# A hybrid encoder step: the scan's eight quads taken in pairs behind a projection's end, whole matmul triples in the first 21 groups, and three smaller moves

## The chip, the cores and the metric

The kernel runs on one core of a Trainium2 chip. The metric is the device time of one execution in microseconds; the time of a kernel is the median of its runs. PE is TensorE (matmuls), ACT is ScalarE, DVE is VectorE, POOL is GpSimd, SP is SyncE, which issues most DMAs.

## The reference

One layer (DEPTH = 1) of a streaming encoder runs for two request groups with the same weights: 256 prompt frames and 32 sample frames, 288 token columns in all.

```python
xn   = rmsnorm(x, norm_mix_pre)
u, z, xbc, dt_raw = split(xn @ w_in)          # 2048 -> 1024 | 2048 | 2560 | 32
y_pool = pool_mixer(u)                        # trailing means of 2/4/8/16, minus u, @ w_pool, * pool_scale
xbc  = silu(causal_dwconv(xbc, width 4))      # -> xs (2048), B and C (2 groups x 128)
y    = scan(xs, softplus(dt_raw + bias), -exp(a_log), B, C) + D * xs    # 32 heads of 64
y_ssd = group_rmsnorm(y * silu(z)) * ssd_norm
x    = x + rmsnorm(concat[y_pool, y_ssd] @ w_out, norm_mix_post)
up   = causal_dwconv(rmsnorm(x, norm_ffn_pre) @ w_up, width 3)          # 2048 -> 2 x 5632
x    = x + rmsnorm((silu(gate) * value) @ w_down, norm_ffn_post)
```

It returns x for both groups and the new histories and scan states.

The exact scan of the prompt is computed here for each head as a masked product: with g the running sum of dt * A, token row s contributes exp(g_t - g_s) * (C_t . B_s) * dt_s * x_s to every later token t. The sample tokens take the same product over their own rows and a product with the old state.

## The kernel before

**Projections.** Each of the big products (w_in, w_out, w_up, w_down) is made by `project` in groups of 256 output columns. Tokens are the moving operand (288 columns), weights the stationary one. The weights come from HBM as `raw` (SP), ACT rounds them to a high half `whi`, and DVE subtracts to get the low half `wlo`; four buffers of each. The tokens are split in the same way. `mm3` makes one product of 128 x 128 weights as a triple of matmuls: high weights with high tokens, high weights with low tokens, low weights with high tokens. A weight *part* is what one whi/wlo tile feeds: 24 matmuls. A w_in group has 2048 rows and 256 columns, so four parts, 96 matmuls. Groups 1 to 8 are xs (the scan's input; B, C and two of the eight u tiles are made in the start stage), 9 to 16 are z, 17 to 19 are u, 20 to 25 are w_out (group 20 holds two column groups), and from 26 on come w_up and w_down. The table `TURNED` says for some groups in which of their parts the triple is turned (high-high, low-high, high-low).

**The scan.** The 32 heads are taken in eight *quads* of four. `ssd_first(q)` fetches the quad's row of running sums, broadcast to all partitions (`gb`, read from `g_d` by POOL), and the old state (`h0t`, SP), and makes `ce`, the decay towards the old state. `ssd_tokens(q)` reads the tokens transposed (`xk`, from `xs_d`). `ssd_quad(q)` scales xk by dt (DVE), makes the mask `m`: 12 ACT activations, one ACT exponential over all, one DVE product with `cbt` (the product of C and B), and then 16 float32 matmuls into two PSUM tiles `py`, one for each pair of heads, and two DVE additions of D * xs. `m`, `gb`, `ce` have two buffers, `xk` three. [...]

**Order.** The program is written by a tile scheduler: an instruction goes as early as its priority and the estimated readiness of its inputs allow; `pin` fixes matmuls in the order written, and the whi/wlo splits run ahead of their use by priority. `XS_RATE` and `Z_RATE` say behind which xs and z group a quad is written. Between matmuls that aren't pinned the scheduler may put others, so a quad's 16 may stand in the middle of a part and between the three matmuls of a triple.

**Start.** The first six column tiles (0 and 1 of u, 2 to 5 of B and C) are made from chunks of rows of `w_first` as they land, `CHUNKS` = six of one 128-row slice and five of two; `prepare` splits them into one tile `w` with the high and the low half, `W_GAP` elements apart. Twelve matmuls on `busy` run ahead of the first data. The sum of squares of the tokens is made by matmuls with a square of ones (`prs`).

Of the kernel before, what the change touches and what calls it, by code (L numbers as in the profile page):

```python
# [8 lines left out]
F32 = mybir.dt.float32  # L9
F32R = mybir.dt.float32r  # L10
# [6 lines left out]
P = 128  # L17
TC = {"schedule_with_timeline_sim": True}
D_MODEL = 2048
NP_ = 256  # L20
# [43 lines left out]
def body(  # L64
# [69 lines left out]
    def split_w(raw, kb, nk, nc_, after=()):  # L134
# [13 lines left out]
            out.append([(kb + k + i, hi[:, i, :], lo[:, i, :]) for i in range(n)])  # L148
        return out

    def mm3(out, wh, wl, a, start, stop, other=False):
        pairs = [(wh, 0), (wh, 1), (wl, 0)]
        if other:
            pairs[1:] = pairs[:0:-1]
        for n, (w, x) in enumerate(pairs):
            pe.matmul(out, w, a[:, x, :], start=start and n == 0, stop=stop and n == 2)  # L156

    groups_done = [0]

    def project(view, groups, acts, ksplit, before=None, done=None, spare=(), hold=(), behind=None, wait=(), tail=()):  # L160
# [7 lines left out]
        turned = TURNED.get(groups_done[0])  # L168
        n_part = 0
        after = before(*ksplit[0]) if before else None  # L170
        for i, (kb, n) in enumerate(ksplit):
            raws = [fetch_w(view, kb, n, c0, w) for c0, w in groups]
            nxt = None
            if before and i + 1 < len(ksplit):
                nxt = before(*ksplit[i + 1])
            m0 = 0
            for raw, (c0, w) in zip(raws, groups):
                parts = split_w(raw, kb, n, w, tuple(wait) + ((after or ()) if m0 else ()) + (hold if i else tail if m0 + w // P == n_all else ()))
                for q, part in enumerate(parts):
                    for m in range(w // P):  # L180
                        c = slice(m * P, (m + 1) * P)
                        with ExitStack() as order:
                            if behind and part[-1][0] == k_last and m0 + m > SUMS_AFTER:
                                order.enter_context(tc.issue_after(behind[-1].ins))
                            for k, hi, lo in part:
                                mm3(accs[m0 + m], hi[:, c], lo[:, c], acts[k], k == k_first, k == k_last, n_part == turned)
# [22 lines left out]
    busy = xin.tile([P, 2 * P], F32R, name="busy")  # L209
    pin(dve.memset(busy.bitcast(F32), 1.0))  # L210
    win = w_in
    O_Z, O_X = D_POOL, D_POOL + D_SSD
# [39 lines left out]

    ones = const.tile([P, P], F32, name="ones")
    pool.memset(ones, 1.0)
    eps_t = side1.tile([P, 1], F32, name="eps_t")
    pool.memset(eps_t, EPS)
    warm = const.tile([P, 1], F32, name="warm")
# [26 lines left out]
        pin(pe.matmul(first[1][:, : 2 * P], busy[:, 0:P], busy, start=True, stop=True))  # L284
    last_split = []
    lows = []
    sq2 = xin.tile([P, 2 * NT], F32, name="sq2")

    def prepare(i):

# [53 lines left out]
    for i, (kb, n) in enumerate(CHUNKS):  # L344
        if i + 1 < len(CHUNKS):
            ahead_w.append(prepare(i + 1))
            for q in SQUARES.get(i + 1, ()):
                squares(q)
        if i == 5:
            first_load(10)  # L350
            pin(dve.memset(ebuf[0][:, 0:1], 0.0))
# [12 lines left out]
        products = [  # L364
            (r, m, k, x) for m in (2, 3, 4, 5, 0, 1) for k in range(n) for r, x in ((0, 0), (0, 1), (1, 0))
        ]
        if i == 0:
            products.sort(key=lambda q: (q[1] < 2, q[0], q[3]))
        for q, (r, m, k, x) in enumerate(products):
            if i == len(CHUNKS) - 2 and q == 24:  # L370
                p_ = aux([P, NT], "prs")
                for c in (slice(0, NT), slice(NT, 2 * NT)):
                    pin(pe.matmul(p_, busy[:, 0:P], sq_r[:, c], start=c.start == 0, stop=c.start > 0))
# [5 lines left out]
            pin(pe.matmul(  # L379
                first[m], w[r][:, k, m * P : (m + 1) * P], xn[kb + k][:, x, :],  # L380
                start=kb + k + r + x == 0, stop=kb + k == KD - 1 and r == 1,
            ))
# [26 lines left out]
    ones_r = const.tile([P, P], F32R, name="ones_r")  # L409
    pin(act.activation(ones_r, ones, AF.Copy))  # L410
    sc_stage = const.tile([P, 2, 3, NXC], F32, name="sc_stage")
    np_stage = const.tile([P, 2, 15, NU], F32, name="np_stage")
    hist_c = col["hist_c"].rearrange("p (r t) -> p r t", t=NXC)
# [198 lines left out]
        pool.dma_start(out=xk[:, 2, :], in_=xs_d[q][TAIL:, :])  # L612
        tokens[q] = xk

    def ssd_quad(q):


        gi = q // 4
# [19 lines left out]
            dve.tensor_tensor(m, m, cbt[:, gi : gi + 1, :].broadcast_to([P, 4, MW]), op=ALU.mult)  # L638
        )

        ys = []
        for i in range(2):
            y = aux([P, NT], "py")
            ys.append(y)
            for k in range(4):
                for j in range(2):
                    h = 2 * i + j
                    c = slice(64 * j, 64 * j + 64)
                    f_ = slice(64 * h, 64 * h + 64)
                    if k == 0:  # L650
                        ins = pe.matmul(y[c, 0:256], xw[:, 0, f_], m[:, h, 0:256], start=True, stop=False)  # L651
                    elif k == 1:
                        ins = pe.matmul(y[c, 128:256], xw[:, 1, f_], m[:, h, 256:384], start=False, stop=True)  # L653
                    elif k == 2:
                        ins = pe.matmul(y[c, 256:], xw[:, 2, f_], m[:, h, 384:], start=True, stop=False)  # L655
                    else:
                        ins = pe.matmul(y[c, 256:], h0t[:, i, c], ce[:, h, :], start=False, stop=True)  # L657
                    if i or k or j:
                        tc.keep_in_program_order(ins)
        if q + 1 < NX // 2:  # L660
            ssd_first(q + 1)
        for i in range(2):
            t = 2 * q + i
            dve.scalar_tensor_tensor(xs[t], xs[t], dcol[:, t : t + 1], ys[i], op0=ALU.mult, op1=ALU.add)

    def token_sums(p_, sq, first_, last_, pin=False):

# [97 lines left out]
    done = [-1]  # L765
    rg = []

    def run_quads(n):
        for _ in range(n):
            if quads and 2 * quads[0] + 1 < len(xs):  # L770
                done[0] = 2 * quads[0] + 1
                ssd_quad(quads.pop(0))

    def run_gates():
        while gates and gates[0] in zs and gates[0] <= done[0]:
# [2 lines left out]
    for i in range(1, NX // 2):  # L778
# [2 lines left out]
        ps = project(win, [(O_X + 256 * i, 256)], xn, K16)  # L781
        xs_evac(i, ps)
        xs_conv(i - 1)
        run_quads(XS_RATE[i])
    for i in range(NX // 2):
        if Z_RATE[i]:
            ssd_tokens(quads[0])
# [7 lines left out]
        run_quads(Z_RATE[i])  # L795
        for j in range(2):
            gate_silu(2 * i + j)
        run_gates()
# [4 lines left out]
    run_quads(NX)  # L803
# [8 lines left out]
    assert not gates and not quads  # L812


    ups = [project(win, [(512, 256)], xn, K16)]
# [198 lines left out]
    state_ops = {}  # L1014
    last_ops = []

    def mix_before(g):
        def hook(kb, n):
            if g == 0 and kb == 0:
                pool_group(1)  # L1020
                pool_group(0)
        return hook
# [399 lines left out]
```

## Time and profile before

| | us |
|---|---|
| median of 3 runs | 1307.47 (1307.16 to 1308.04) |
| the profiled execution | 1308.33 |
| its span in the profile | 1306.6 |
| PE busy | 1299.5 (99% of the span) |
| DVE busy | 894.7 (68%) |
| ACT busy | 672.8 (51%) |
| POOL busy | 244.8 (19%) |
| start stage, until the first matmul of `project` | 47.66 |
| scan: first and last start of a quad's first matmul | 126.1 and 254.6 |

The granted TensorE clock is 0.999 over the span. Busy time of PE is modelled from starts, so a busy PE need not be at its best pace; the distance between starts of matmuls is read from the chain of waits (duration of a piece by its count) and from the windows view (matmuls that overlap a stretch).

### The profile page before, as it was taken

How to read it: one execution, taken by the hardware profiler on the slowest of the kernel's cores; microseconds unless marked ns; L12 is line 12 of the kernel's file. 1: busy time of each engine (PE TensorE's matmuls, PEld its weight loads, DVE VectorE, ACT ScalarE, POOL GpSimd, SP SyncE). 2: the span in 40 equal slices, each digit the busy share in tenths (PEclk: the TensorE clock that was granted, in tenths of full speed). 3: DMA queues.
4: the chain of work that ended last, by engine and by line, in shares of the span. 5: the costliest groups of instructions: out<-in, count | busy, mean ns of one | idle time of the engine just before them, and what ended most of it. 6: DMA issues, size and time to landing. Idle time of an engine off the chain costs nothing.

```text
span 1306.6 us, 25261 instructions
## 1 busy us (share of the span) xinstructions
PE 1299.5 (99%) x10043; PEld 1289.3 (99%) x10043; DVE 894.7 (68%) x1515; ACT 672.8 (51%) x1013; POOL 244.8 (19%) x399
## 2 busy tenths in 40 slices
PE   9999999999999999999999999999999999999998
PEld 9999999999999999999999999999999999999997
DVE  7999988879645588977766643345666666754454
ACT  7557767446544566544444433334444444444442
POOL 2342212222222221211211100001111111201110
PEclk9999999999999999999999999999999999999999
DMA  9568875445666468766554445455544554466653
GB/s 345 187 212 278 292 218 182 162 153 201 213 218 212 154 198 259 214 186 190 174 171 162 157 174 171 158 180 174 182 162 162 175 174 169 162 233 188 212 180 115
DMA packets 110038, 251.75 MB, mean 193 GB/s; under 512 B 64736, under 2 KB 73856, under 8 KB 87392
## 3 DMA queue, kind: packets, MB, share of 16 engines
q1 hardware_dynamic: 103568, 233.36, 54.7%
q0 software_dynamic: 5824, 16.13, 4.1%
q8 instruction: 78, 1.28, 0.4%
q10 hardware_dynamic: 528, 0.66, 0.2%
q14 instruction: 40, 0.33, 0.1%
HBM read 237.11 MB, written 13.00 MB: 191 GB/s over the span
## 4 chain that ended last, share of the span: by engine, by line
PE 98%; DVE 0%; DMA 0%; ACT 0%; ACTq 0%; issue 0%
PE acc L156 91%; PE acc L379 2%; PE acc_x L156 1%; PE acc_x L379 1%; PE py L651 1%; PE acc L1283 0%; PE acc L1284 0%; PE py L653 0%; DMA raw<-in_w_first 0%; PE acc_t L1306 0%; PE pst L992 0%; PE acc L386 0%; DVE rm L1046 0%; PE py L657 0%; PE py L655 0%
## 5 line engine op out<-in xcount | busy, mean ns | idle before, releaser
L147 DVE TENSOR_TENSOR wlo<-raw,whi 128x1024 fp32r<-128x1024 f32 (+1 forms) x396 | 473.0, 1196 | 303.3 <-ACT whi L146 302.3
L146 ACT ACTIVATE whi<-raw 128x1024 fp32r<-128x1024 f32 (+1 forms) x396 | 408.2, 1032 | 466.6 <-PE acc L156 375.6
L156 PE MATMUL acc<-hn,whi 128*128 128x288 f32 x2752 | 538.6, 294 | 0.4 <-ACT hn L1059 0.4
L156 PEld LDWEIGHTS acc<-hn,whi 128*128 128x128 f32 x2752 | 436.4, 188 | 1.0 <-ACT hn L1059 0.9
L156 PE MATMUL acc<-hn,wlo 128*128 128x288 f32 x1376 | 399.7, 291 | 0.0
L156 PEld LDWEIGHTS acc<-hn,wlo 128*128 128x128 f32 x1376 | 258.9, 188 | 0.0
L156 PE MATMUL acc<-fa,whi 128*128 128x288 f32 x1320 | 257.5, 293 | 0.0
L156 PE MATMUL acc<-xn,whi 128*128 128x288 f32 x1216 | 239.1, 294 | 0.0
L156 PEld LDWEIGHTS acc<-fa,whi 128*128 128x128 f32 x1320 | 208.9, 188 | 0.0
L156 PEld LDWEIGHTS acc<-xn,whi 128*128 128x128 f32 x1216 | 193.1, 188 | 0.7 <-issue 0.5
L156 PE MATMUL acc<-fa,wlo 128*128 128x288 f32 x660 | 192.1, 291 | 0.0
L156 PE MATMUL acc<-xn,wlo 128*128 128x288 f32 x608 | 177.6, 293 | 0.0
L156 PEld LDWEIGHTS acc<-fa,wlo 128*128 128x128 f32 x660 | 124.3, 188 | 0.0
L1109 POOL COPY fc_stage<-ebuf 128x4 f32<-128x4 f32 x88 | 26.4, 299 | 471.6 <-DVE ebuf L1108 450.7
L156 PEld LDWEIGHTS acc<-xn,wlo 128*128 128x128 f32 x608 | 114.4, 188 | 0.1
L156 PE MATMUL acc<-mixs,whi 128*128 128x288 f32 x512 | 100.5, 294 | 0.0
L1115 DVE SCALAR_TENSOR_TENSOR fc<-ebuf,cols,fc 128x290 f32<-128x290 f32 x176 | 90.4, 517 | 3.9 <-ACT fc L1113 1.1
L1113 ACT ACTIVATE fc<-ebuf,cols 128x290 f32<-128x290 f32 x88 | 54.4, 623 | 73.2 <-DVE ebuf L1108 71.1
L1104 POOL COPY ebuf<-cols 128x2 f32<-128x2 f32 x88 | 69.9, 794 | 108.4 <-DVE fc L1115 96.0
L156 PEld LDWEIGHTS acc<-mixs,whi 128*128 128x128 f32 x512 | 81.3, 188 | 0.0
L156 PE MATMUL acc<-mixs,wlo 128*128 128x288 f32 x256 | 74.1, 293 | 0.0
L156 PE MATMUL acc<-mixp,whi 128*128 128x288 f32 x256 | 50.2, 293 | 0.0
(322 smaller groups left out, 1241.0 us busy)
## 6 DMA issues: line engine op xcount, KB each, us to landing
raw<-in_w_up SPq DMA_DIRECT2D x80, 1024.0 KB, 5.1
raw<-in_w_in SPq DMA_DIRECT2D x38, 1024.0 KB, 5.2
raw<-in_w_down SPq DMA_DIRECT2D x32, 1024.0 KB, 4.9
raw<-in_w_out SPq DMA_DIRECT2D x24, 1024.0 KB, 5.1
raw<-in_w_down SPq DMA_DIRECT2D x16, 768.0 KB, 4.2
raw<-in_w_up SPq DMA_DIRECT2D x14, 512.0 KB, 4.4
gb<-g_d POOLq DMA_DIRECT2D x8, 832.0 KB, 5.8
raw<-in_w_first SPq DMA_DIRECT2D x5, 768.0 KB, 12.3
```

Source lines behind the costliest of these rows:

```text
L146: act.activation(hi, raw[:, k : k + n, :], AF.Copy)
L147: dve.tensor_tensor(lo, raw[:, k : k + n, :], hi.bitcast(F32), op=ALU.subtract)
L156: pe.matmul(out, w, a[:, x, :], start=start and n == 0, stop=stop and n == 2)
L379: pin(pe.matmul(first[m], w[r][:, k, m * P : (m + 1) * P], xn[kb + k][:, x, :], start=kb + k + r + x == 0, stop=kb + k == KD - 1 and r == 1,))
L651: ins = pe.matmul(y[c, 0:256], xw[:, 0, f_], m[:, h, 0:256], start=True, stop=False)
L1104: pool.tensor_copy(e[:, 258:260], hist_f[:, :, i])
L1109: pool.tensor_copy(fc_stage[:, :, :, i], e[:, 256:324].rearrange("p (s c) -> p s c", c=34)[:, :, 0:2])
L1113: act.activation(c, e[:, 0:290], AF.Identity, bias=col["f_b"][:, i : i + 1], scale=f_w[:, 0, i : i + 1])
L1115: dve.scalar_tensor_tensor(c, e[:, r_ : r_ + 290], f_w[:, r_, i : i + 1], c, op0=ALU.mult, op1=ALU.add)
```

## The change

1. **Pairs.** `ssd_quad` is split into `ssd_masks` (xk, masks), `ssd_products` (the 16 matmuls, all pinned) and `ssd_add`. `run_masks` is called behind some groups as before (`XS_RATE`, `Z_RATE`), but the products of two quads are made together by `run_pair`, called behind the last xs group and behind z groups 1, 4 and 6 (counted from 0). The two quads' 256 prompt columns stand in one bank each, side by side for the two head pairs, and the sample columns of both in a third (`py_s`), so a pair needs three aux banks. The additions are cut into prompt and sample columns.
2. **Whole triples.** In groups 1 to 21 `mm3` runs low-high, high-high, high-low, and the second and third are pinned to the first. `TURNED` is new, and may name several parts.
3. **Start.** Chunk 0 is sorted so that column tiles 2, 3 have all three products first, then 4, 5, then 0, 1; chunks 4 and 5 are turned; W_GAP is 48; the sum of squares uses `ones_r` instead of `busy`, which shares a buffer with the squares.
4. **w_pool.** The first two of w_pool's four groups move from before w_out's first slice to the place between the two column groups of its second slice; the last slice of w_out's first group is cut into two of four.

On PE, behind the 24th weight part and after the eighth xs group. In before (lines 156, 651 to 657) the first quad, each row a run of equal matmuls:

```order
417 L156 MATMUL acc<-xn,whi 128x288 x2
418 L156 MATMUL acc<-xn,wlo 128x288
419 L156 MATMUL acc<-xn,whi 128x288 x4
420 L651 MATMUL py<-m,xk 64x256 x2
421 L653 MATMUL py<-m,xk 64x128 x2
422 L655 MATMUL py<-m,xk 64x32 x2
423 L657 MATMUL py<-ce,h0t 64x32 x2
427 L657 MATMUL py<-ce,h0t 64x32 x2
428 L156 MATMUL acc<-xn,wlo 128x288
429 L156 MATMUL acc<-xn,whi 128x288 x2
```

In after (165, 673 to 679) the first pair; the four product rows stand there four times:

```order
545 L165 MATMUL acc<-xn,wlo 128x288
546 L165 MATMUL acc<-xn,whi 128x288 x2
547 L673 MATMUL py<-m,xk 64x256 x2
548 L675 MATMUL py<-m,xk 64x128 x2
549 L677 MATMUL py_s<-m,xk 64x32 x2
550 L679 MATMUL py_s<-ce,h0t 64x32 x2
562 L679 MATMUL py_s<-ce,h0t 64x32 x2
563 L165 MATMUL acc<-xn,wlo 128x288
564 L165 MATMUL acc<-xn,whi 128x288 x2
```

A quad stood inside a triple's run and now two stand between whole triples, later in the program (behind part 32 instead of part 24).

On DVE, around the mask product of quad 0 (xk is the token tile of a quad, ebuf, conv and xs are the convolution of a projection's output). Before:

```order
205 L439 SCALAR_TENSOR_TENSOR conv<-ebuf_169,pah,conv 128x291
206 L147 TENSOR_TENSOR wlo<-raw,whi 128x1024
207 L444 SCALAR_TENSOR_TENSOR xs<-tanh,conv 128x256
208 L445 SCALAR_TENSOR_TENSOR xs<-tanh,conv 128x32
209 L197 STREAM_TRANSPOSE blocks<-xs 128x288
210 L638 TENSOR_TENSOR m<-m,cbt 128x1664
211 L628 TENSOR_TENSOR xk<-xk,tok 128x768
212 L147 TENSOR_TENSOR wlo<-raw,whi 128x1024
```

And after:

```order
203 L454 SCALAR_TENSOR_TENSOR conv<-ebuf_169,pah,conv 128x291
204 L454 SCALAR_TENSOR_TENSOR conv<-ebuf_170,pah,conv 128x291
205 L152 TENSOR_TENSOR wlo<-raw,whi 128x1024
206 L653 TENSOR_TENSOR m<-m,cbt 128x1664
207 L643 TENSOR_TENSOR xk<-xk,tok 128x768
208 L152 TENSOR_TENSOR wlo<-raw,whi 128x1024
```

The wlo of row 208 is the one for part 23, which stood ahead of the mask product (row 206) before.

On ACT the `ce` of quad 1 stood behind the twelve mask rows of quad 0 (rows 83 to 94 of before):

```order
82 L601 ACTIVATE ce<-gb 128x128
83 L633 ACTIVATE m<-gb,tok 128x256
94 L633 ACTIVATE m<-gb,tok 128x32
95 L601 ACTIVATE ce<-gb 128x128
96 L633 ACTIVATE m<-gb,tok 128x256
```

and now stands ahead of them, so it needs the second gb; 24 mask rows of two quads follow, with one whi after the sixteenth:

```order
76 L616 ACTIVATE ce<-gb 128x128
79 L616 ACTIVATE ce<-gb 128x128
81 L648 ACTIVATE m<-gb,tok 128x256
96 L648 ACTIVATE m<-gb,tok 128x256
97 L151 ACTIVATE whi<-raw 128x1024
98 L648 ACTIVATE m<-gb,tok 128x128
106 L651 ACTIVATE m<-m 128x1664
107 L151 ACTIVATE whi<-raw 128x1024
```

On SP's queue the store of `g_d` moves from behind eight stores of xs_d to behind five of them, and on POOL's the two `gb` reads move from behind the second xk to ahead of it.

The diff, cut to its core:

```diff
-XS_RATE = (0, 0, 1, 0, 1, 0, 1, 0)
-Z_RATE = (1, 0, 1, 1, 0, 1, 1, 0)
+XS_RATE = (0, 0, 1, 0, 1, 0, 0, 1)
+Z_RATE = (1, 0, 1, 1, 1, 1, 0, 0)
+PAIR_XS = (7,)
+PAIR_Z = (1, 4, 6)
...
-W_GAP = 16
-W_ROOM = 32
+W_GAP = 48
+W_ROOM = 64
+TURNED_FIRST = (4, 5)
+WHOLE = range(1, 22)
 TURNED = {
-    1: 0, 5: 3, 7: 2, 8: 1, 10: 1, 12: 1, 13: 1, 15: 1, 16: 1, 18: 1, 20: 8, 22: 0, 27: 0, 28: 1, 46: 0, 65: 0,
+    1: (0,), 5: (3,), 9: (0,), 11: (0,), 14: (0,), 15: (0,), 16: (0,), 18: (0,), 20: (0, 8), 22: (0,), 27: (0,),
+    28: (1,), 46: (0,), 65: (0,),
 }
...
     def mm3(out, wh, wl, a, start, stop, other=False):
         pairs = [(wh, 0), (wh, 1), (wl, 0)]
+        if whole[0]:
+            pairs = pairs[2:] + pairs[:2]
         if other:
             pairs[1:] = pairs[:0:-1]
         for n, (w, x) in enumerate(pairs):
-            pe.matmul(out, w, a[:, x, :], start=start and n == 0, stop=stop and n == 2)
+            ins = pe.matmul(out, w, a[:, x, :], start=start and n == 0, stop=stop and n == 2)
+            if n and whole[0]:
+                pin(ins)
...
-            for r, x in ((0, 0), (0, 1), (1, 0))
+            for r, x in (((0, 0), (1, 0), (0, 1)) if i in TURNED_FIRST else ((0, 0), (0, 1), (1, 0)))
         ]
         if i == 0:
-            products.sort(key=lambda q: (q[1] < 2, q[0], q[3]))
+            products.sort(key=lambda q: ((q[1] + 4) % 6 // 2, q[0], q[3]))
...
+        if q % 2 == 0:
+            ssd_first(q + 1)
+        return xw, m, h0t, ce
+
+    def ssd_products(q, sample, xw, m, h0t, ce):
+
+        rows_ = aux([P, 2 * NP_], "py")
...
+    def run_pair():
+        sample = aux([P, 4 * NS], "py_s")
+        ys = {q: ssd_products(q, sample, *masks_[q]) for q in sorted(masks_)}
+        if quads:
+            ssd_first(quads[0])
+        for q in ys:
+            ssd_add(q, ys[q])
+            masks_.pop(q)
+            done[0] = 2 * q + 1
...
         xs_conv(i - 1)
-        run_quads(XS_RATE[i])
+        if i in PAIR_XS:
+            run_pair()
+        run_masks(XS_RATE[i])
...
-            w_out, [(256 * c, 256) for c in grp], mix, [(8, 8), (16, 8), (0, 8)],
-            mix_before(grp[0]), lambda m, p_: mix_out(p_),
+            w_out, [(256 * c, 256) for c in grp], mix, [(8, 8), (16, 8), (4, 4), (0, 4)] if not grp[0] else [(8, 8), (16, 8), (0, 8)],
+            done=lambda m, p_: mix_out(p_), middle=None if grp[0] else first_groups,
```

More of the change, by code (lines that the diff above doesn't have):

```diff
@@ L149, in split_w @@
         return out
+    whole = [False]
     def mm3(out, wh, wl, a, start, stop, other=False):
         pairs = [(wh, 0), (wh, 1), (wl, 0)]
+        if whole[0]:
+            pairs = pairs[2:] + pairs[:2]
         if other:
@@ L155, in mm3, with project @@
         for n, (w, x) in enumerate(pairs):
-            pe.matmul(out, w, a[:, x, :], start=start and n == 0, stop=stop and n == 2)
+            ins = pe.matmul(out, w, a[:, x, :], start=start and n == 0, stop=stop and n == 2)
+            if n and whole[0]:
+                pin(ins)
     groups_done = [0]
-    def project(view, groups, acts, ksplit, before=None, done=None, spare=(), hold=(), behind=None, wait=(), tail=()):
+    def project(view, groups, acts, ksplit, before=None, done=None, spare=(), hold=(), behind=None, wait=(), tail=(), middle=None):
         n_all = sum(-(-w // P) for _, w in groups)
@@ L167, in project @@
         groups_done[0] += 1
-        turned = TURNED.get(groups_done[0])
+        turned = TURNED.get(groups_done[0], ())
+        whole[0] = groups_done[0] in WHOLE
         n_part = 0
@@ L176, in project @@
             m0 = 0
-            for raw, (c0, w) in zip(raws, groups):
+            for r, (raw, (c0, w)) in enumerate(zip(raws, groups)):
+                if middle and (i, r) == (1, 1):
+                    middle()
                 parts = split_w(raw, kb, n, w, tuple(wait) + ((after or ()) if m0 else ()) + (hold if i else tail if m0 + w // P == n_all else ()))
@@ L185, in project @@
                             for k, hi, lo in part:
-                                mm3(accs[m0 + m], hi[:, c], lo[:, c], acts[k], k == k_first, k == k_last, n_part == turned)
+                                mm3(accs[m0 + m], hi[:, c], lo[:, c], acts[k], k == k_first, k == k_last, n_part in turned)
                         if done and i + 1 == len(ksplit) and q + 1 == len(parts):
@@ L208, in body @@
     xin = start.enter_context(tc.tile_pool(name="xin", bufs=1))
-    busy = xin.tile([P, 2 * P], F32R, name="busy")
+    busy = xin.tile([P, 2 * NT], F32R, tag="sq", bufs=1, name="busy")[:, : 2 * P]
     pin(dve.memset(busy.bitcast(F32), 1.0))
@@ L254, in body @@
     pool.memset(ones, 1.0)
+    ones_r = const.tile([P, P], F32R, name="ones_r")
     eps_t = side1.tile([P, 1], F32, name="eps_t")
@@ L286, in body @@
     lows = []
-    sq2 = xin.tile([P, 2 * NT], F32, name="sq2")
+    sq2 = xin.tile([P, 2 * NT + 16], F32, name="sq2")[:, : 2 * NT]
     def prepare(i):
@@ L350, in body @@
             first_load(10)
+            pin(act.activation(ones_r, ones, AF.Copy))
             pin(dve.memset(ebuf[0][:, 0:1], 0.0))
@@ L364, in body @@
         products = [
-            (r, m, k, x) for m in (2, 3, 4, 5, 0, 1) for k in range(n) for r, x in ((0, 0), (0, 1), (1, 0))
+            (r, m, k, x) for m in (2, 3, 4, 5, 0, 1) for k in range(n)
+            for r, x in (((0, 0), (1, 0), (0, 1)) if i in TURNED_FIRST else ((0, 0), (0, 1), (1, 0)))
         ]
         if i == 0:
-            products.sort(key=lambda q: (q[1] < 2, q[0], q[3]))
+            products.sort(key=lambda q: ((q[1] + 4) % 6 // 2, q[0], q[3]))
         for q, (r, m, k, x) in enumerate(products):
@@ L372, in body @@
                 for c in (slice(0, NT), slice(NT, 2 * NT)):
-                    pin(pe.matmul(p_, busy[:, 0:P], sq_r[:, c], start=c.start == 0, stop=c.start > 0))
+                    pin(pe.matmul(p_, ones_r, sq_r[:, c], start=c.start == 0, stop=c.start > 0))
                 rstd = const.tile([P, NT], F32, tag="spread", bufs=3, name="rstd")
@@ L408, in body @@
         dve.tensor_copy(sel64, sel.unsqueeze(2).broadcast_to([HEADS, 2, 64]))
-    ones_r = const.tile([P, P], F32R, name="ones_r")
-    pin(act.activation(ones_r, ones, AF.Copy))
     sc_stage = const.tile([P, 2, 3, NXC], F32, name="sc_stage")
@@ L613, in ssd_tokens, with ssd_masks @@
         tokens[q] = xk
-    def ssd_quad(q):
+    def ssd_masks(q):
         gi = q // 4
@@ L639, in ssd_quad @@
         )
+        if q % 2 == 0:
[3 more added lines that the diff above has]
+        rows_ = aux([P, 2 * NP_], "py")
         ys = []
         for i in range(2):
-            y = aux([P, NT], "py")
-            ys.append(y)
+            y, y_s = rows_[:, NP_ * i : NP_ * (i + 1)], sample[:, NS * (2 * (q % 2) + i) :][:, :NS]
+            ys.append((y, y_s))
             for k in range(4):
@@ L654, in ssd_quad, with ssd_add @@
                     elif k == 2:
-                        ins = pe.matmul(y[c, 256:], xw[:, 2, f_], m[:, h, 384:], start=True, stop=False)
+                        ins = pe.matmul(y_s[c, :], xw[:, 2, f_], m[:, h, 384:], start=True, stop=False)
                     else:
[L657 to L661, printed above, removed]
+                        ins = pe.matmul(y_s[c, :], h0t[:, i, c], ce[:, h, :], start=False, stop=True)
+                    pin(ins)
+        return ys
+    def ssd_add(q, ys):
         for i in range(2):
             t = 2 * q + i
-            dve.scalar_tensor_tensor(xs[t], xs[t], dcol[:, t : t + 1], ys[i], op0=ALU.mult, op1=ALU.add)
+            for c, y in zip((slice(0, NP_), slice(NP_, NT)), ys[i]):
+                o = xs[t][:, c]
+                dve.scalar_tensor_tensor(o, o, dcol[:, t : t + 1], y, op0=ALU.mult, op1=ALU.add)
     def token_sums(p_, sq, first_, last_, pin=False):
@@ L766, in body, with run_masks @@
     rg = []
-    def run_quads(n):
+    masks_ = {}
+    def run_masks(n):
         for _ in range(n):
-            if quads and 2 * quads[0] + 1 < len(xs):
-                done[0] = 2 * quads[0] + 1
-                ssd_quad(quads.pop(0))
+            q = quads.pop(0)
+            masks_[q] = ssd_masks(q)
+    def run_pair():
[7 more added lines that the diff above has]
+            done[0] = 2 * q + 1
     def run_gates():
@@ L794, in body @@
             rg.append(rstd_all(gsum[0], 0.25 / 1024, "rg0", sq_parts(mp)))
-        run_quads(Z_RATE[i])
+        if i in PAIR_Z:
+            run_pair()
+        run_masks(Z_RATE[i])
         for j in range(2):
@@ L802, in body @@
                 dve.tensor_tensor(xs[t], xs[t], rg[0], op=ALU.mult)
-    run_quads(NX)
     run_gates()
@@ L811, in body @@
             )
-    assert not gates and not quads
+    assert not gates and not quads and not masks_
     ups = [project(win, [(512, 256)], xn, K16)]
@@ L1015, in body, with first_groups @@
     last_ops = []
[L1017 to L1022, printed above, removed]
+    def first_groups():
+        pool_group(1)
+        pool_group(0)
     for grp in ((0, 1), (2,), (3,), (4,), (5,), (6, 7)):
         project(
-            w_out, [(256 * c, 256) for c in grp], mix, [(8, 8), (16, 8), (0, 8)],
-            mix_before(grp[0]), lambda m, p_: mix_out(p_),
+            w_out, [(256 * c, 256) for c in grp], mix, [(8, 8), (16, 8), (4, 4), (0, 4)] if not grp[0] else [(8, 8), (16, 8), (0, 8)],
+            done=lambda m, p_: mix_out(p_), middle=None if grp[0] else first_groups,
         )
```

## The prediction

> **What bounds the kernel now.** I read the page first, then the waits of PE, then the chain of waits in order of time.
>
> ```profile
> span 1306.6 us, 25261 instructions
> PE 1299.5 (99%) x10043; PEld 1289.3 (99%) x10043; DVE 894.7 (68%) x1515; ACT 672.8 (51%) x1013; POOL 244.8 (19%) x399
> PE 98%; DVE 0%; DMA 0%; ACT 0%; ACTq 0%; issue 0%
> PE acc_x L284 <- DVE busy L210: 1.3, 1, 1.3
> PE py__15339 L1348 <- ACT diag L1347: 1.0, 1, 1.0
> PE acc L156 <- ACT hn L1059: 0.4, 1, 0.4
> 515.92 763.10 PE acc L156 x5868
> ```
>
> TensorE is busy for 99% of the span, holds 98% of the chain, and waits for other engines three times, 2.7 us in all. So there is no wait to win: the time is the sum of the distances between starts of matmuls, and the change can only shorten that sum (fewer matmuls at an awkward place, a shorter distance) or put a new wait into it. The last row gives the pace of a quiet stretch: 763.10/5868 = 130.0 ns for each matmul of 288 columns, or 3.12 us for a weight part of 24.
>
> The same pace isn't held everywhere. The windows view of PE counts the matmuls that overlap a stretch:
>
> ```profile
> 72.00:97.00 25.00, 25.00 (x194) 1.00 0.68 212
> 309.00:337.00 28.00, 28.00 (x213) 1.00 0.65 219
> 341.00:366.00 25.00, 25.00 (x194) 1.00 0.52 177
> ```
>
> 25 us at 130.0 ns hold 192.3, so the count is 1.7 above the whole ones. 28 us hold 213 - 1.7 = 211.3, which is 132.5 ns each, with PE busy throughout and the clock at 1.00. So there are two paces, a good one and one about 2.5 ns slower, and in the slow stretch (w_pool and the head of w_out) a w_out triple is cut open by other matmuls. I read the slow pace as a matter of the order in which high and low weights alternate after such a cut; this is my reading, no row names it.
>
> Between 108 and 145 us the scan cuts into the projection:
>
> ```profile
> 108.97 17.21 PE acc L156 x131
> 126.17 0.58 PE py L651 x4
> 126.76 0.22 PE py L653 x4
> 126.98 0.09 PE py L655 x4
> 127.06 0.12 PE py L657 x4
> 127.18 0.46 PE py L651 x4
> 127.64 0.22 PE py L653 x4
> 127.86 0.09 PE py L655 x4
> 127.95 0.12 PE py L657 x4
> 128.06 5.56 PE acc L156 x40
> ```
>
> One quad (16 float32 matmuls) is 128.06 - 126.17 = 1.89 us. Its first L651 row has 0.58 against 0.46 for the second: 0.12 us is the entry. Behind it 40 projection matmuls take 5.56 where 40 x 130 ns are 5.20: 0.36 us, which I split (estimate) into 0.2 for the way out of the float32 matmuls and 0.16 for two parts at the slow pace (24 x 2.5 ns = 0.06 us each, 0.08 with the last one).
>
> **The change part by part.** The sum is made against the profiled execution, 1308.33 us, which is 0.86 above the median of the timed runs (1307.47) and 1.7 above its span.
>
> *Pairs.* The quads' matmuls are the same in number and shape. Eight entries and ways out become four: 4 x (0.12 + 0.2) = **-1.3 us**. From below, if the way out is none of it, -0.5; from above, if all of the 0.36 goes, -1.9.
>
> *Whole triples, and where they are turned.* A pair now stands between whole triples at a group's start, and the w_pool matmuls stand between w_out's column groups. If the slow stretch goes, it gives 28.00 - 211.3 x 0.130 = 0.53 us, and at its edges some 0.1 more; the parts behind the quads give 0.16 x 2 more (two of the eight quads were left in the slow pace). The turned parts are about as many as before. **-0.9 us**, between 0 (order does nothing) and -1.2. [...]
>
> *The first chunks.*
>
> ```profile
> 4.74 0.42 ACT w L323
> 5.21 2.77 PE acc L379 x10
> 7.98 1.44 PE acc_x L379 x6
> 9.42 2.06 PE acc L379 x12
> 12.27 1.57 PE acc L379 x12
> ```
>
> Before, PE stands at the low half of chunk 0's columns until ACT's part ends at 5.16; now all products of columns 2 and 3 come first, and I expect some 0.45 us less standing there. Up to 10 us a matmul takes 1.44/6 = 240 ns (the clock isn't up), later 131, so 0.45 us of earlier cold work is 1.9 matmuls, worth 1.9 x 131 = 0.25 us. The warm chunks go at 131 ns; with chunks 4 and 5 turned the 180 matmuls of chunks 6 to 10 may go at 130, 0.2 us less, against two turned chunks. **-0.3 us**, between 0 and -0.6. [...]
>
> *The queues around quads 0 and 1.* This is what the change adds. On ACT the second ce now stands ahead of every mask row, and on DVE one weight part's low half stands behind the masks of quad 0 and the xk of quad 1. Before:
>
> ```profile
> 111.05 3.71 ACT L633 ACTIVATE m<-gb,tok 128x256 f32<-128x256 f32 x12
> 114.67 0.29 ACT L601 ACTIVATE ce<-gb 128x128 f32<-128x128 f32 x1
> 116.68 1.04 ACT L146 ACTIVATE whi<-raw 128x1024 fp32r<-128x1024 f32 x1
> 119.27 1.58 ACT L636 ACTIVATE m<-m 128x1664 f32<-128x1664 f32 x1
> 117.76 1.23 DVE L147 TENSOR_TENSOR wlo<-raw,whi 128x1024 fp32r<-128x1024 f32 x1 [1.04 <-ACT whi L146]
> 120.88 1.89 DVE L638 TENSOR_TENSOR m<-m,cbt 128x1664 f32<-128x1664 f32 x1 [0.95 <-ACT m L636]
> 122.69 0.95 DVE L628 TENSOR_TENSOR xk<-xk,tok 128x768 f32<-128x768 f32 x1
> 101.27 0.38 SPq L533 DMA_DIRECT2D g_d<-g  x1
> 95.32 5.84 SPq L200 DMA_DIRECT2D xs_d<-blocks  x8
> 105.08 1.06 POOL L597 DMA_DIRECT2D gb<-g_d  x2
> DMA to landing us min/median/max: 4.3/5.8/9.0
> ```
>
> DVE already stood 0.95 us ahead of the mask product at 120.88, but the low half that PE needed next (117.76) was ahead of that. Now it is behind. Let L be the landing of the second gb. From L on, ACT has ce 0.29, a conv (0.6), 24 mask rows at 3.71/12 (7.4), one whi (1.04) and the exponential (1.58); DVE follows with the product 1.89, the xk 0.95 and the low half 1.23. Less the overlap of neighbours (0.1 each) that is L + 14.6. PE comes to that part at about 108.97 + 17.21 - 24 x 0.13 - 0.6 = 122.4. So PE stands L - 107.8, if that is positive. For L: g_d is stored after five of the eight xs_d stores, so at 95.32 + 5 x 0.73 = 99.0 instead of 101.27; it lands some 2 us later, and the two gb are issued at about 101.0 and 101.6 (they no longer stand behind the second xk on POOL's queue). They land 4.3 to 9.0 us later, 5.8 in the median: L is between 106 and 110.6. The wait is 0 to 2.8; by the median 0, by the longest of the eight 2.8; I take **+1.0 us**, nearer the median. What waits behind it on PE is everything. [...]
>
> The three later pairs have the same form: two quads' masks, 2 x (3.71 + 1.58 + 0.29) = 11.2 us of ACT, come together once the pair before them has freed both m buffers, where before 8 us or more lay between two quads. The order spreads whi among them. Bounds 0 (no PE wait at any quad before) and 2.8 each; I take **+0.8 us** for the three. If PE stands once, the next parts may go at the slow pace until a turned part (up to 9 x 0.06): **+0.2**.
>
> *At nothing:* the scan's additions become four for a quad (32-column pieces apart) instead of two, the sum of squares uses ones_r, busy shares a buffer. They are DVE and ACT work beside a PE that needs neither at once (DVE 68% busy); if that cover is gone, each added 0.2 us would show one for one, 16 x 0.2 = 3.2 us at the utmost.
>
> **Sum:** -1.3 - 0.9 - 0.3 + 1.0 + 0.8 + 0.2 = -0.5: 1307.8 for a profiled execution and, 0.86 lower, **1307.0 us** for the median.
>
> **The rivals.**
> 1. *Faster: the masks never keep PE waiting, and the slow pace goes.* -1.3 - 1.2 - 0.6 = -3.1: 1307.47 - 3.1 = 1304.4. [...] For it: the median landing gives a wait of 0. Against: the 24 rows ahead of one low half. [...]
> 2. *Slower: the low-first triple sets the slow pace.* Groups 1 to 21 now run low, high, high. Where projection matmuls begin with a low one after float32 work (128.06), the stretch was over 130 ns. If whole triples do that for all of the 75 or so parts from 100 us to the first group that isn't pinned, 1800 x 2.5 ns = 4.5 us: 1307.47 - 1.3 - 0.3 + 4.5 = 1310.4, and 1311.4 with the gb wait. It decides from some 1700 matmuls at the slow pace on (1300 with the gb wait). Against: a turned part behind each pair changes the order again, and the steady cycle of low, high, high is that of high, high, low.
> 3. *Slower: each pair's masks hold up the low halves.* 2.8 for the first and 1.5 for each of three more, 7.3: 1307.47 - 2.5 + 7.3 = 1312.3. For it: ACT's 11.2 us at once. Against: no wait at any quad before. It decides where a whi comes over 6 us late.
> 4. *Order does nothing.* 1307.0 + 0.9 = 1307.9, no change.
>
> **How the numbers follow.** A measurement of this kernel tells about 0.2% (2.6 us) from no change. My forecast has 0.40, rival 1 0.26, rival 2 0.14, rival 3 0.10, rival 4 0.10. Faster by over 0.2%: rival 1, 0.26. Within: forecast and rival 4, 0.50. Slower: rivals 2 and 3, 0.24. The forecast's own range is 1305 to 1309.5 (gb wait 0 to 2.8). The range takes in rival 1 up to the earlier clock and rival 2 short of its worst: 1303.4 to 1311.0.
>
> **What would show it.** Right: the four pairs at about 3.86 us each, way in and out included, in the chain of waits; a PE wait on DVE's wlo of 0 to 2.8 us near 122 us behind a DVE idle ahead of m<-m,cbt; 309 to 337 us with some 217 matmuls instead of 213. Wrong: no PE wait and a span under 1303; a span of 1310 with PE busy all the time and 25-us windows of the first 21 groups holding 190 instead of 194 (rival 2); waits of over 1.5 us ahead of two or more pairs (rival 3).

## The result, and the profile after

The changed kernel is slower: 1315.65 us median (1315.09 to 1316.27) against 1308.0 for the kernel before in the same comparison (1307.16 to 1308.21), a ratio of 1.0059 (95% interval 1.0048 to 1.0069). The profiled execution took 1315.38 us with a span of 1313.6, so 7.0 us more span than before. The page (span, busy time, the chain by engine), then PE's waits (us in total, times, longest):

```profile
span 1313.6 us, 25271 instructions
...
PE 1303.0 (99%) x10043; PEld 1292.4 (98%) x10043; DVE 899.0 (68%) x1531; ACT 672.2 (51%) x1013; POOL 249.2 (19%) x399
...
PE 92%; DMA 3%; issue 2%; DVE 1%; ACT 1%; POOL 0%; SPq 0%; POOLq 0%; ACTq 0%
```

```profile
PE acc L165 <- DVE wlo L152: 3.3, 2, 3.0
```

As many matmuls keep PE busy 3.5 us longer, and there is 3.3 us of a wait that the kernel before had not. Of what makes up the 7.0 us the prediction had the wait's mechanism and the pairs; the pace was a rival; what followed the wait was not in it. "Low-first" below means triples that begin with the low weights, as in the changed kernel, "high-first" those that begin with the high ones, as before.

**The wait.** The chain of waits leads from the second gb to the low half of part 23, as the prediction had it (start, length, what):

```profile
97.44 3.92 DMA g_d<-g
...
102.17 8.69 DMA gb<-g_d
...
110.88 0.04 ACT ce L616
...
113.22 3.42 ACT m L648 x11
116.64 0.95 ACT whi L151
...
117.78 2.12 ACT m L648 x7
119.90 1.50 ACT m L651
...
123.23 0.79 DVE xk L643
...
124.10 1.23 DVE wlo L152
...
125.37 30.81 PE acc L165 x216
```

The gb landed at 110.86. L - 107.8 gives 3.06 us; PE's timeline shows 3.00 in front of its matmul at 125.37. The landing sets the size of the wait: issued at 102.17, 8.69 us long, near the 9.0 that was the longest of the eight before. That the issue came so near the predicted 101.6 is luck in part: the store of g_d went out earlier than predicted (97.44 instead of 99.0) and took longer (3.92 us instead of some 2), two errors that cancel.

**Behind the wait.** The windows view of PE just behind it (matmuls and granted clock):

```profile
122.00:125.40 3.40, 0.40 (x4) 1.00 0.85 317
...
126.00:129.30 3.30, 3.30 (x16) 0.50 0.91 278
129.30:132.00 2.70, 2.70 (x22) 0.99 0.29 74
```

From 126.0 to 129.3 us the granted clock is 0.50 and matmuls start 240 ns apart. The trace has 1.6 us of excess over 130 ns per matmul there that isn't slow pace. The wait cost its own 3.0 us and these 1.6 us.

**The pace.** Stretches of 102 matmuls around 300 us, before and after, which hold no scan and no wait:

```profile
295.11 13.26 PE acc L156 x102
```

```profile
286.36 13.58 PE acc L165 x102
...
300.74 13.60 PE acc L165 x102
```

13.26/102 is 130.0 ns, 13.60/102 is 133.3. Summed from the starts in the trace, part by part, 48 of the first 98 parts have an excess of 0.07 to 0.11 us in the changed kernel (4.1 us together), 8 in the kernel before (0.7). These are called slow parts below; a part at 130 ns is at the good pace.

**Pairs and start.** A pair runs as one block:

```profile
156.18 0.58 PE py L673 x4
...
159.72 0.12 PE py_s L679 x4
159.83 19.37 PE acc L165 x144
```

159.83 - 156.18 = 3.65 us against 2 x 1.89 = 3.78, and a way out of 0.10 instead of two of 0.12: four pairs save 0.5 and 0.5 us, 1.0. The start ends earlier (before 47.66):

```profile
44.63 2.08 PE acc L403 x32
46.71 13.39 PE acc L165 x101
```

The span's 7.0 us are then: start -0.95, waits +3.3, half clock +1.6, slow pace +3.4, pairs -1.0, the first parts of w_up behind 480 us +0.35 (the ninth run, whose matmuls are there those of the kernel before, has a step of that size too, so it need not be the change); 0.3 stays unassigned.

### The profile page after: what moved, and what is told of

The parts are those of the page before. It is cut to its first block, busy times and chain, and to the rows that moved or that the text cites. A ratio compares the mean times of both kernels' runs of the same rounds, so it can differ in the third digit from the quotient of the medians.

```text
span 1313.6 us, 25271 instructions
## 1 busy us (share of the span) xinstructions
PE 1303.0 (99%) x10043; PEld 1292.4 (98%) x10043; DVE 899.0 (68%) x1531; ACT 672.2 (51%) x1013; POOL 249.2 (19%) x399
## 4 chain that ended last, share of the span: by engine, by line
PE 92%; DMA 3%; issue 2%; DVE 1%; ACT 1%; POOL 0%; SPq 0%; POOLq 0%; ACTq 0%
PE acc L165 88%; DMA raw<-in_w_first 1%; PE acc_x L165 1%; DMA gb<-g_d 1%; PE py L673 1%; ACT m L648 1%; PE acc L1319 0%; DVE w L333 0%; PE acc L1320 0%; PE acc_t L1342 0%; DMA mg<-in_x_g 0%; DMA xg<-in_x_g 0%; DMA g_d<-g 0%; DVE sq L353 0%; PE py L675 0%
## 5 line engine op out<-in xcount | busy, mean ns | idle before, releaser
L165 PE MATMUL acc<-xn,whi 128*128 128x288 f32 x1216 | 242.5, 296 | 0.0
L165 PEld LDWEIGHTS acc<-xn,whi 128*128 128x128 f32 x1216 | 195.8, 189 | 0.0
L165 PE MATMUL acc<-xn,wlo 128*128 128x288 f32 x608 | 180.9, 297 | 3.3 <-DVE wlo L152 3.3
```

The costliest lines, as they stand in the source:

```text
L165: ins = pe.matmul(out, w, a[:, x, :], start=start and n == 0, stop=stop and n == 2)
```

## The experiments

**First, the order inside a triple.** The edit, on the changed kernel:

```diff
-        if whole[0]:
-            pairs = pairs[2:] + pairs[:2]
```

> The changed kernel with its whole triples in the old order (high-high, high-low, low-high) in groups 1 to 21; all else as changed. Theory A (low-first triples fall into the slow pace and the turned parts don't bring them out): nearly all of the 58 slow parts at +0.08 us go, so about 4.5 us less than the changed kernel, near 1311, with the 3.0 us wait at 122 us and the half clock behind it still there. Theory B (the wait and the half clock behind it start the slow pace): the parts behind 125 us stay slow, near 1315. Theory C (pinning or the pairs make it slow, not the order inside a triple): slow as before, near 1315.

1308.72 us (1.0002 of before, 0.9992 to 1.0011), with a span of 1306.2, 7.4 less than the changed kernel's. The slow parts fell from 48 to 17, 2.5 us; the same stretch as above in the chain of waits, and the only wait on a weight half:

```profile
294.19 13.26 PE acc L163 x102
```

```profile
PE acc L163 <- ACT whi L151: 0.5, 1, 0.5
```

But the 3.0 us wait and the half clock went too, which no theory had said. DVE's queue shows why:

```profile
116.51 1.22 DVE L152 TENSOR_TENSOR wlo<-raw,whi 128x1024 fp32r<-128x1024 f32 x1 [1.17 <-ACT whi L151]
...
119.64 1.89 DVE L651 TENSOR_TENSOR m<-m,cbt 128x1664 f32<-128x1664 f32 x1 [0.95 <-ACT m L649]
```

The low half of part 23 stands ahead of the mask product again, as before the change. With its first matmul free and high, the scheduler writes another order on ACT and DVE: the order of the triple moved the queues as well. So this run doesn't separate the wait from the pace. It shows that together they are 7.4 us of span; the next two separate them.

**Second, the wait alone.** Quad 1's decay and masks are held behind the high and low half of part 23, low-first triples stay:

```diff
-XS_RATE = (0, 0, 1, 0, 1, 0, 0, 1)
+XS_RATE = (0, 0, 1, 0, 0, 1, 0, 1)
...
+        if q == 1:
+            with tc.issue_after(splits[-1].ins), tc.issue_after(whis[-1].ins):
+                ssd_first(1)
+                return mask_rows(q)
+        return mask_rows(q)
```

> The changed kernel with quad 1's decay and mask rows held behind the whi and wlo of part 23, so that this low half no longer stands behind 24 mask rows and the second gb. Both theories: the 3.0 us wait at 122 us and the half clock behind it (1.6 us) go. Theory A: the slow pace from 289 to 370 us and after the pairs stays, so 4.9 us less, near 1310.7. Theory B: parts 24 to 43 come back to 130.0 ns as well, another 1.6 us or more, 1309 or lower.

1311.22 us (1.0021, 1.0011 to 1.0030), with a span 4.8 less than the changed kernel's:

```profile
PE acc L167 <- DVE wlo L154: 0.6, 1, 0.6
```

```profile
295.85 13.60 PE acc L167 x102
```

The wait and the half clock are 4.8 us of the loss, net of a wait of 0.6 us that this run has itself; the pace did not come back (45 slow parts). Theory B, that the stop of PE starts the slow pace, falls for these parts: they are slow without the 3.0 us wait, and from 112 us on, ahead of the 0.6 us one at 132. That a stop can never start it is not shown; the eighth and ninth runs bear on that.

**Third, both edits.**

> Both edits together: high-first whole triples and quad 1's masks behind part 23. Theory A: no wait, no half clock, good pace: 1315.6 - 4.9 - 4.5 = about 1306.2, below the kernel before (1308.0) by the start (0.95) and the pairs (1.3) less what the w_pool move costs. Theory B or C: as the second run, 1309 to 1311.

1307.28 us (0.9990, 0.9981 to 0.9999): a miss by 1.1 us. But this is the plainest test of the pace: against the second run only the order inside the triples is edited (the queues may move with it, as in the first run), the time falls by 3.9 us (3.0 of span, which includes the second run's 0.6 us wait) and the slow parts from 45 to 17. I took the 17 for those in which high-first triples with a free first matmul are opened by other matmuls; the seventh run tests that.

**Fourth, the start alone, on the kernel before.** The edit is part 3 of the change, with nothing else of it.

> The kernel before with the start's edits alone: chunk 0's new order, chunks 4 and 5 turned, the gap of 48, ones_r for the sum of squares. If the start's 0.95 us (47.66 to 46.71 at the first matmul of a projection) belong to these edits alone, 1307.1 and a first projection matmul at 46.7 us; if they come from later parts of the order, 1308.0.

1307.97 us against 1308.61 in the same comparison (0.9997, 0.9988 to 1.0007): in the times no more than a hint. In its trace the first projection matmul starts at 46.53 us and the span is 1305.8, 0.8 less. PE's windows show where it comes from; before:

```profile
6.00:8.00 2.00, 2.00 (x10) 1.00 1.04 363
8.00:10.00 2.00, 2.00 (x10) 1.00 1.01 373
```

and in the changed kernel:

```profile
6.00:8.00 2.00, 2.00 (x15) 1.00 0.95 350
8.00:10.00 2.00, 2.00 (x17) 1.00 1.00 359
```

```profile
7.39 13.31 DMA raw<-in_w_first
```

The clock column reads 1.00 in all four, so it's the count that shows it: the matmuls came up from 240 to 130 ns almost 4 us earlier (at 6.5 instead of 10.4 us), which alone would be worth some 1.8 us (an estimate: 16 matmuls at 240 instead of 130 ns). The chain of waits of the start no longer stands on PE but on the landing of the rows of w_first (last row), which takes part of the gain back.

The earlier pace is not the edit's doing, though. The ninth run has the start of the kernel before, and the eleventh has the new one; their windows and the end of the start stage are

```profile
6.00:8.00 2.00, 2.00 (x15) 1.00 1.04 374
46.94 23.14 PE acc L161 x176
...
6.00:8.00 2.00, 2.00 (x10) 1.00 0.98 367
47.07 23.01 PE acc L160 x175
```

The old start comes up to pace early in the ninth run's trace and late in the trace before, and the new one late in the eleventh's. So the moment varies from one execution to another. With the pace up early, the old start ends at 46.94 us and the new one at 46.71 (changed kernel) or 46.53 (this run): by these the edits are worth 0.2 to 0.4 us of the 0.95 (an estimate), and the rest is the moment at which the matmuls came up to pace.

**Fifth, the form of the turned part.** On the second run's kernel:

```diff
-        if whole[0]:
+        if whole[0] and not other:
             pairs = pairs[2:] + pairs[:2]
```

> The second run's kernel (low-first whole triples, quad 1's masks held back) with the turned parts in the form of the kernel before (high-high, low-high, high-low), the rest of the triples low-first. In the second run the turned part (low-high, high-low, high-high) was followed by the slow pace in 6 of 9 cases. Theory A1 (the form of the turned part decides where the pace lands): slow parts fall from 45 to under 10, 3 us less, near 1308. Theory A2 (low-first triples land in the slow pace whatever stands ahead of them): the same count of slow parts, near 1311.

1313.38 us (1.0039, 1.0025 to 1.0052): slower still. 72 parts are slow, some at 0.107 us, and the first turned part at 47 us already leaves the slow pace behind it. Theory A1 falls, and theory A2 had expected 1311 and no more slow parts than in the second run.

**Sixth, no turned part.**

```diff
 TURNED = {
-    1: (0,), 5: (3,), 9: (0,), 11: (0,), 14: (0,), 15: (0,), 16: (0,), 18: (0,), 20: (0, 8), 22: (0,), 27: (0,),
+    1: (0,), 22: (0,), 27: (0,),
```

> The second run's kernel without any turned part in groups 2 to 21. If a turned part is the only way back to the good pace and low-first entries land in the slow one, every part from the nineteenth on is slow: 79 x 0.08 = 6.3 us instead of 3.6, less nine turned parts at 0.05: 2.2 us more, near 1313.4. If the turned parts themselves bring the slow pace, the parts behind the pairs stay at 130.0 and it is 3 us less, near 1308.

1312.11 us (1.0029, 1.0018 to 1.0041), 0.9 above the second run (1.7 by the spans), where 2.2 were expected. In its trace none of the parts from 105 to 370 us is at the good pace, and 69 are slow parts by the count used here:

```profile
297.57 13.60 PE acc L167 x102
...
333.57 39.20 PE acc L167 x294
```

13.60/102 and 39.20/294 are 133.3 ns. So once the pace was slow, none of the four low-first entries behind pairs brought it back, and a low-first turned part gets out only sometimes: counted part by part, the part behind a turned one was at the good pace in 2 of 10 cases in the changed kernel and 3 of 10 in the second run, in 11 of 11 in the kernel before.

The order of the matmuls doesn't settle it alone, however. The fourth run's kernel has the matmuls of the kernel before from the first projection on, yet behind the quad at 239 to 241 us one part is slow in it (high-first in both; before, then the fourth run):

```profile
240.79 12.75 PE acc L156 x96
...
239.66 12.85 PE acc L157 x96
```

The eleventh run shows that slow part too. So something finer than the order takes part in it; no run here isolates it.

**Seventh and eighth, high-first and whole.** All but the first matmul of a part pinned, without and with the second run's held masks:

```diff
-        if whole[0]:
-            pairs = pairs[2:] + pairs[:2]
...
-            if n and whole[0]:
+            if whole[0] and (n or not free):
                 pin(ins)
```

> The changed kernel with high-first triples kept whole: all three matmuls pinned but for the first of each part. Against the first run (high-first, where the first matmul of a triple was free and 129 matmuls of the first groups stood in opened triples; 33 here). Theory A: the +0.09 stretches at 124 to 150, 166 to 176 and 196 to 212 us of the first run go, 1.5 us less, near 1306.8. If opened triples cost nothing, 1308.7.

> The same with quad 1's masks held behind part 23. The third run had 0.25 us more excess in the projections than the kernel before and came out at 1307.3; with its opened stretches (about 1.2 us) gone, near 1306, 2 us below the kernel before: 1.0 from the start, 1.0 from the pairs. If pairs give nothing, 1307.

1307.99 us (0.9997, 0.9988 to 1.0006) and 1308.16 (0.9999, 0.9990 to 1.0008): both missed. The opened matmuls fell from 129 to 33, but the slow parts only from 17 to 16 and 15, so opened triples are not what makes most of them slow. And a wait came at quads 4 and 5 (eighth run):

```profile
PE acc L165 <- DVE wlo L154: 0.7, 1, 0.7
```

The mask bursts of the later pairs, which cost nothing in the changed kernel, do cost when the rest is closer packed. The eighth run's parts are at the good pace ahead of this wait (130 ns) and slow behind it (134 ns), up to the next pair: here the slow pace did begin at a stop, with high-first triples. What the stop alone does is not shown.

**Ninth, waits of several lengths.** On the kernel before, some low halves made late:

```diff
+REPEAT = {180: 7, 210: 9, 240: 10, 270: 11, 300: 12, 330: 14}
...
+                for _ in range(REPEAT.get(n_split[0], 1)):
-                dve.tensor_tensor(lo, raw[:, k : k + n, :], hi.bitcast(F32), op=ALU.subtract)
+                    dve.tensor_tensor(lo, raw[:, k : k + n, :], hi.bitcast(F32), op=ALU.subtract)
```

> The kernel before, with the subtraction that makes a low half repeated 7, 9, 10, 11, 12 and 14 times (1.2 us each) at the 180th, 210th, 240th, 270th, 300th and 330th weight part of the whole kernel, so that PE is made to wait there by lengths that differ by 1.2 to 2.4 us; the result of the product is the same. If a wait of PE costs its own length alone, the matmuls behind each wait start 130 to 140 ns apart. If a wait of some length brings the half clock, as behind the 3.0 us wait of the changed kernel (14 matmuls at 240 ns, 1.6 us), the matmuls behind the longer waits start 240 ns apart for up to 3.4 us and those behind the shorter don't.

1338.9 us, with the added work. Three of the six places made PE wait. The timeline and then the windows of PE at the shortest of them:

```profile
625.87 0.79 PE L161 MATMUL acc<-hn,whi 128*128 128x288 f32 x4 [0.54 <-ACT whi L149]
628.13 0.40 PE L161 MATMUL acc<-hn,wlo 128*128 128x288 f32 x1 [1.47 <-DVE wlo L152]
```

```profile
628.60:632.00 3.40, 3.40 (x17) 0.53 0.08 31
```

Two waits of 0.54 and 1.47 us within 3 us were followed by the half clock (0.53) for about 3.4 us; the two longer groups of waits (812 to 819 and 1002 to 1013 us) were followed by it for 3.3 and 4.9 us, the latter

```profile
1012.90:1017.80 4.90, 4.90 (x21) 0.50 0.83 239
```

Behind the single waits of 0.6 us (second run) and 0.7 us (eighth) the distances stayed below 140 ns, but for the first matmul's 0.24 us. Which lengths between these bring the half clock, these runs don't show.

This run also has the slow pace, where there is neither a low-first triple nor a float32 block; before, then this run:

```profile
840.00:865.00 25.00, 25.00 (x194) 1.00 0.47 158
...
840.00:865.00 25.00, 25.00 (x188) 1.00 0.54 177
```

From 824 to 1046 us and from 1130 us to the end nearly every part has an excess of 0.11 us, 118 parts in all, against none there before. The first stretch follows stops of PE, the second doesn't; the delayed low halves have opened triples ahead of both, so this run doesn't tell a stop from a changed order as the cause.

**Tenth, all odd quads held.** The eighth kernel with `if q % 2:` in place of `if q == 1:` and one more turned part, 8: (1,).

> The eighth run's kernel (high-first whole triples, pairs, the new start) with the masks of every odd quad held behind the last weight part split at that place, and one more turned part (group 8, part 1). The eighth run has 0.7 us of waits on a low half at 202 us and slow parts behind it until the next turned part, 1.3 us together, and three slow parts at 140 us, 0.2 us. If both go, 1.4 us less: 1306.7 against 1308.15, below the kernel before by more than the interval. If the wait only moves to another pair, 1308.

1306.21 us against 1308.44 (0.9984, 0.9975 to 0.9993): faster than both kernels. PE waits for no low half (the longest wait on a projection's matmul is 0.4 us), 9 parts are slow:

```profile
PE acc L165 <- ACT hn L1100: 0.4, 1, 0.4
...
PE acc L165 <- ACT whi L153: 0.2, 1, 0.2
```

```profile
292.63 13.26 PE acc L165 x102
```

**Eleventh, the same without pairs.** The fourth kernel with high-first whole triples, single quads and the old turned parts.

> The kernel before with the new start and high-first triples kept whole in groups 1 to 21, but with its eight single quads, its old turned parts and w_pool where it was. Against the fourth run (new start alone, 1308.0) the triples opened by quads go: parts 24, 25 and 28 are at the good pace or at most behind a low-first entry, 0.3 us less, and the w_pool stretch stays as it is: 1307.7. If the pairs are what makes the tenth run 2.2 us faster than before, this one stays 1.2 us or more above it (1307.5 or more); if whole high-first triples are, it comes to within 0.5 us of it, 1306.7 or less.

1308.11 us against 1308.73 (0.9996, 0.9987 to 1.0005). It is not within 0.5 us of the tenth: the ratios differ by 0.0012, 1.6 us, though their intervals overlap, and the spans by 2.2 (1307.0 and 1304.8), of which 0.6 is the start stage, the same edit in both. So the pairs, with the fewer turned parts that they need and the place of w_pool, are worth one to two microseconds once nothing waits for their masks; 1.0 of it is read from the chain, and w_pool's place wasn't tried alone.

## Why the prediction was wrong, point by point

- *What bounds the kernel*: right. PE has stayed the bound, and the loss is waits and distances.
- *Pairs, -1.3*: right in mechanism, 1.0 measured. The way out of a block is 0.10 to 0.12 us, not 0.2; the rest of that 0.36 was slow pace.
- *Whole triples, -0.9*: the step that failed. I let the slow stretches go because triples were whole and because "a turned part behind each pair changes the order again". The quads' own row (128.06) had shown a low-first entry in the slow pace, and the diff makes every triple of 21 groups low-first. Wholeness was not the point: low-first and whole gave 45 to 72 slow parts (second, fifth and sixth runs), high-first and whole 9 to 16 (seventh, eighth and tenth). +3.4 instead of -0.9. The turned part, which in the kernel before always brought the good pace, does so in 2 of 10 cases when the triple runs low-first. That the order inside the triple is behind the loss is shown (third against second run); why an entry lands in one pace or another stays open.
- *Start, -0.3*: -0.95 in this pair of traces, but about right for the edits, which are worth 0.2 to 0.4 us where the matmuls come up to pace early in both (fourth run). The rest is the earlier pace; it comes to the old start as well (ninth run), so here it was luck. That the 240 ns of the first microseconds are a clock that isn't up was my reading: the granted clock reads 1.00 there. And no run shows the earlier clock's amount that the lower end of the range, 1303.4, allows for: the runs showed 130 ns from 6.5 us on in one execution and from 10.4 us on in another, and a start stage 0.95 us shorter with the early pace and the edits together.
- *Queue, +1.0*: mechanism, place and formula (L - 107.8) held to 0.1 us, the issue time by two errors that cancel; I took a landing near the median of eight where the same transfer at the same place had taken 8.96. With that row the term is 2.8.
- *What follows a wait*: missing. I priced a stop of PE at its length and 0.2 us. Its 3.0 us cost 1.6 more through the half clock. Here 3.0 us of idle, and 2.0 us in two pieces (ninth run), were enough, and the slow spells lasted 3.3 to 4.9 us.
- *Later pairs, +0.8*: 0 in the changed kernel (two small steps between 171 and 182 us are 0.3 together), 0.7 in the eighth run.
- *Rivals*: rival 2 is what happened to the pace; I gave it 0.14, and priced it with a wait of 1.0 us at most, where wait and half clock were 4.9. Rival 2 and the first wait of rival 3 were counted as one or the other, where both follow from the same low-first pins: with a free, high first matmul the scheduler put the low half ahead of the masks (first run). The range ended at 1311.0; the two at once, 1307.47 - 2.0 + 3.4 + 3.3 + 1.6, are 1313.8, still short of the measured 1315.65.

## What to carry to other kernels

When TensorE is the bound and never waits, look at how matmuls enter: which half comes first in a triple went here with the distance of hundreds of matmuls behind it (130.0 or 133.3 ns, 3.4 us in all), and a pin on the order also moves the queues that feed it. A wait of TensorE can cost more than its length: here one of 3.0 us cost 1.6 us on top, and one of 2.0 us in two pieces was followed by 3.4 us at a granted clock of 0.53, while behind single ones of 0.6 and 0.7 us the distances stayed below 140 ns. Before crediting a gain in the first microseconds to an edit, look at a second execution of the old kernel. And take the landing of a DMA from the same transfer at the same place, not from the median. Two causes that hang on one edit are added, not chosen between.

## What the runs showed of the hardware

Projections of 288 columns ran here at one of three distances on average, 130.0 ns (13.26 us for 102, before), 133.3 (13.60 for 102, changed kernel) or 134.5 (some parts of the fifth run), which is 0, 0.08 and 0.107 us per part of 24, and mostly kept it over long stretches (39.20 us for 294 matmuls in the sixth run). What in the junction of two triples chooses between them stayed open: low-first and high-first triples are the same cycle, and still a turned part leads to different paces (the good one behind 11 of 11 before, behind 2 of 10 in the changed kernel), and the same order of matmuls has led to two paces (12.75 and 12.85 us for 96, before and fourth run). A wait of 3.0 us was followed by 3.3 us at a granted clock of 0.50 (changed kernel), waits of 2.0 us in two pieces by 3.4 us at 0.53 (ninth run). In the same start stage the windows from 6 to 8 us held 15 matmuls in one execution and 10 in another (ninth run and the kernel before).
